# Moving the SBUF places of a split-precision decoder's matmul operands: weight high parts level with the streamed operand, low parts 64 bytes below it

## The chip, the cores and the metric

The kernel runs on one NeuronCore of a Trainium2 chip. The metric is the device time of one execution in microseconds (us). Before the change the median of three runs is 2209.86 us (2209.11 to 2210.26).

## What is computed

The reference is a small decoder trunk in float32: 256 positions, width 2048, two layers. Layer 0 mixes with sliding-window attention, layer 1 with a gated linear recurrence; each is followed by a gated feed-forward block of inner width 6144 with a three-tap causal convolution. Cut to the matrix products that matter here:

```python
def reference(x, ...):                       # x: (1, 256, 2048)
    for layer in range(2):
        h = rmsnorm(x, mix_norm[layer])
        if layer == 0:                       # qkv: 2048 -> 3072, w_o: 2048 -> 2048
            x = x + sliding_window_attention(h, w_qkv, q_gain, k_gain, sinks, w_o)
        else:                                # w_in: 2048 -> 4096, w_out: 2048 -> 2048
            x = x + rglru_block(h, w_in, conv_w, conv_b, w_a, b_a, w_i, b_i, lam, w_out)
        h = rmsnorm(x, ffn_norm[layer])      # w_up: 2048 -> 12288, w_down: 6144 -> 2048
        x = x + conv_ffn(h, w_up[layer], conv_w[layer], conv_b[layer], w_down[layer])
    return x
```

## The kernel before

**Split precision.** Every weight and every activation that TensorE multiplies is held as two parts: a high part (the value rounded to the matmul's input format, `F32R`) and a low part (the remainder). A product is the sum of high times high, high times activation-low and low times activation-high. The first two are one matmul: an activation row holds its high and its low part side by side (`h[P, KD, 2, T]`, 512 columns), so streaming the row through the high weights gives both sums in 512 PSUM columns. The third streams only the 256 high columns through the low weights.

**Chunks.** The weights are read in 372 chunks of 1 MB (128 partitions x 2048 numbers, 8192 bytes per partition) in one fixed order: `wk` 4, `wv` 4, `wq` 16, `wo` 16, then `wup` 96 and `wdn` 48 of layer 0, `win` 32, `wout` 16, and `wup` 96 and `wdn` 48 of layer 1. For each chunk SyncE's DMA queue loads `raw`; ScalarE copies it to `hi` (line 115); VectorE subtracts `hi` from `raw` and writes `lo` (line 123). There are three buffers each of `raw`, `hi` and `lo`. A call of `advance()` issues these three steps for the chunk that comes next. They sit between the groups of matmuls, so that each engine's program order interleaves them with the work on the results.

**Matmuls of a chunk.** A chunk holds 16 weight tiles of 128x128. TensorE loads a tile (a weight load) and streams the activation row past it (a matmul); while a matmul streams, the next tile is being loaded. `mm_hi` (line 189) streams 512 columns against `hi`, `mm_lo` (line 195) 256 columns against `lo`. In the stages `wup` (result `pu`), `win` (`px` and `py`), `wq` (`pq`), `wo` (`po`) and `wout` (`pr`) a chunk is a run of 16 matmuls of `mm_hi` and then a run of 16 of `mm_lo`; in `wq` the scores and transposes of the heads before stand inside the run of `mm_hi`. In `wdn` (`pd`) a chunk is 8 `mm_hi`, 8 `mm_lo`, 8 `mm_hi`, 8 `mm_lo`. The streamed operand is `h` for `wup`, `win` and `wq`, `g` (the gated inner values) for `wdn`, `z` (the gated recurrence) for `wout` and `ao` (the attention output) for `wo`.

**Where tiles lie.** Inside a partition the tiles lie one after another in the order in which the pools and tiles are declared, each start rounded up to 32 bytes. In what follows the place of a tile is its start byte modulo 256. A weight tile is 512 bytes, a row of a streamed operand 2048 bytes, a buffer 8192 bytes, so all tiles of a buffer, all three buffers and all rows of an operand have one place. Before the change `x` begins at byte 1152 and `h` at 17,536, which is place 128. The long-lived tiles of the pool `per` end with `sp`, `sp4` and `sp8` (64 bytes each, used for the recurrence's decay), and behind them come `raw`, `hi` and `lo`, and then everything that lives in one stage only, all from place 64 on:

| tile | start byte, before | place, before | place, after |
|---|---|---|---|
| `h` | 17,536 | 128 | 128 |
| `raw` (3) | 62,016 | 64 | 128 |
| `hi` (3) | 86,592 | 64 | 128 |
| `lo` (3) | 111,168 | 64 | 64 |
| `g`, `kz` (attention keys) | 135,744 | 64 | 128 |
| `vh` (attention values) | 152,128 | 64 | 128 |
| `ao` | 160,320 | 64 | 128 |
| `ghi`, `glo`, `xc` (gates) | 168,512, 172,608, 176,704 | 64 | 128 |
| `z` | 184,896 | 64 | 128 |
| `qh`, `pt` (attention, two each) | 218,624, 198,144 | 0 | 32 |

The lines that set this, and the two matmul helpers:

```python
per = ctx.enter_context(tc.tile_pool(name="per", bufs=1))
rawp = ctx.enter_context(tc.tile_pool(name="rawp", bufs=3))
hip = ctx.enter_context(tc.tile_pool(name="hip", bufs=3))
lop = ctx.enter_context(tc.tile_pool(name="lop", bufs=3))
...
pe.matmul(ps, lhsT=hi[:, off + k * n:off + k * n + P],
          rhs=rhs[:, xk].rearrange("p a t -> p (a t)"), ...)      # line 189
...
pe.matmul(ps[:, T:], lhsT=lo[:, off + k * n:off + k * n + P],
          rhs=rhs[:, xk, 0, :], ...)                              # line 195
```

Of the kernel before, what the change touches and what calls it, by code (L numbers as in the profile page):

```python
# [19 lines left out]
F32 = mybir.dt.float32  # L20
F32R = mybir.dt.float32r
AF = mybir.ActivationFunctionType
ALU = mybir.AluOpType
AX = mybir.AxisListType

P = 128
D = 2048
T = 256
KD = D // P
# [11 lines left out]
def trunk(ctx, tc, xT, wq, wk, wv, wo, win, wg, wout, wup, wdn, mixg, ffng, kqg, sinks,  # L41
# [3 lines left out]
    act, dve, pool, pe = nc.scalar, nc.vector, nc.gpsimd, nc.tensor  # L45

    def f(ap):
        return ap.bitcast(F32)

    per = ctx.enter_context(tc.tile_pool(name="per", bufs=1))  # L50
    rawp = ctx.enter_context(tc.tile_pool(name="rawp", bufs=3))
    hip = ctx.enter_context(tc.tile_pool(name="hip", bufs=3))
    lop = ctx.enter_context(tc.tile_pool(name="lop", bufs=3))
    ctx.enter_context(tc.manual_schedule())

    x = per.tile([P, KD, T], F32, name="x")
# [10 lines left out]
    fb = per.tile([P, 2, NT_UP], F32, name="fb")  # L67
    rw = per.tile([P, KD, 4], F32, name="rw")
    rbs = per.tile([P, 4, KD], F32, name="rbs")
    sp = per.tile([P, KD], F32, name="sp")  # L70
    sp4 = per.tile([P, KD], F32, name="sp4")
    sp8 = per.tile([P, KD], F32, name="sp8")


    order = []
# [91 lines left out]
    def rsqrt1(y, v):  # L167

        act.activation(out=y, in_=v, func=AF.Ln)
        act.activation(out=y, in_=y, func=AF.Exp, scale=-0.5)  # L170

    def rsqrt2(y, v, tmp):

        dve.tensor_tensor(out=tmp, in0=v, in1=y, op=ALU.mult)
        dve.scalar_tensor_tensor(out=tmp, in0=tmp, scalar=-0.5, in1=y, op0=ALU.mult, op1=ALU.mult)
        dve.scalar_tensor_tensor(out=y, in0=tmp, scalar=1.5, in1=y, op0=ALU.add, op1=ALU.mult)
# [102 lines left out]
    with ExitStack() as ph:  # L279
        ap_ = ph.enter_context(tc.tile_pool(name="attn", bufs=1, reuse_waits="tile"))  # L280
# [6 lines left out]
        kz = ap_.tile([P, 4, 2, 2, T], F32R, name="kz")  # L287
        vh = ap_.tile([P, 2, 2, 512], F32R, name="vh")
        ao = ap_.tile([P, KD, 2, T], F32R, name="ao")
        kq = ap_.tile([P, 1], F32, name="kq")  # L290
        kg = ap_.tile([P, 2], F32, name="kg")
        snk = ap_.tile([P, 32], F32, name="snk")
        nsnk = ap_.tile([P, 32], F32, name="nsnk")
        cb = ap_.tile([P, T], F32, name="cb")
# [72 lines left out]
        def k_fin(p):  # L367
            s, sq = ksq.pop(p)
            pk = psT.tile([P, 512], F32, tag="pT", name=f"pk{p}")
            pe.matmul(pk[:, 0:T], lhsT=bones, rhs=sq, start=True, stop=True)  # L370
            yield
            v = a2.tile([P, T], F32, tag="ka", name=f"kv{p}")
            r = a2.tile([P, T], F32, tag="kr", bufs=1, name=f"kr{p}")
            t = a2.tile([P, T], F32, tag="kt", bufs=1, name=f"kt{p}")
            dve.scalar_tensor_tensor(out=v, in0=pk[:, 0:T], scalar=1.0 / HD, in1=cb, op0=ALU.mult, op1=ALU.add)
            rsqrt1(r, v)
            yield
            rsqrt2(r, v, t)
            dve.scalar_tensor_tensor(out=s, in0=s, scalar=kq[:, 0:1], in1=r, op0=ALU.mult, op1=ALU.mult)
            for i in range(2):  # L380
                sl = slice(64 * i, 64 * i + 64)
                act.copy(out=kz[sl, p, 0, i, :], in_=s[sl])
                dve.tensor_tensor(out=kz[sl, p, 1, i, :], in0=s[sl], in1=f(kz[sl, p, 0, i, :]), op=ALU.subtract)
# [40 lines left out]
        for c in range(4):  # L424
            hi, lo = use()
            fin = k_fin(c)
            step(fin)
            for kk in range(4):
                k = 4 * c + kk
                for b in range(2):  # L430
                    tb = slice(b * P, b * P + P)
                    wsl = slice(kk * 512, kk * 512 + 512)
                    pe.matmul(pv[b], lhsT=h[:, k, 0, tb], rhs=hi[:, wsl], start=k == 0, stop=False)
                    pe.matmul(pv[b], lhsT=h[:, k, 1, tb], rhs=hi[:, wsl], start=False, stop=False)
                    pe.matmul(pv[b], lhsT=h[:, k, 0, tb], rhs=lo[:, wsl], start=False, stop=k == KD - 1)
            if c == 0:
                k_epi(3, psk[3])
            step(fin)
            dma_next()
            split_hi()  # L440
            if c:
                split_lo()
            finish(fin)
# [520 lines left out]
```

## Time and profile before

| | |
|---|---|
| median of three runs | 2209.86 us |
| the profiled execution | 2210.21 us |
| span of its instructions | 2208.4 us |
| TensorE busy with matmuls | 2184.8 us, 12,656 matmuls |
| VectorE, ScalarE, GpSimd busy | 1568.3, 1178.4, 153.3 us |
| granted TensorE clock over the span | 0.996 |
| read from HBM | 401.06 MB |

How to read it: busy times overlap, since the engines work side by side. Matmuls are pipelined, so the duration that the profile gives for one runs on into the next; the pace is the time from one start to the next, and the pace of a run of matmuls is the difference between the start of its first matmul and the start of the first one after it. The timeline of TensorE merges neighbouring matmuls of one kind: its first column is the start in us, the second the time until the last one of the group has ended, and x16 is their number.

### The profile page before, as it was taken

What the parts mean: (1) busy time and instruction counts of PE and PEld (TensorE: products, weight loads), DVE (VectorE), ACT (ScalarE), POOL (GpSimd) and SP (SyncE); (2) the same over time, 40 slices, a digit from 0 to 9 for tenths busy, and PEclk for the clock granted to TensorE, in tenths of its full rate; (3) what the DMA queues carried; (4) which work ended last, traced back from release to release, by engine and by line L of the source; (5) the groups of instructions that cost most, each with busy time, mean ns of one, the idle gap of its engine ahead of it and who ended that gap; (6) DMA issues with size and microseconds to landing.
All of it is one profiled execution on the core that took longest, in us unless ns stands there. A gap on an engine that the chain in (4) does not pass through costs nothing.

```text
span 2208.4 us, 30710 instructions
## 1 busy us (share of the span) xinstructions
PE 2184.8 (99%) x12656; PEld 1922.3 (87%) x12656; DVE 1568.3 (71%) x1877; ACT 1178.4 (53%) x1426; POOL 153.3 (7%) x140
## 2 busy tenths in 40 slices
PE   7999999999999999999999999999999999999999
PEld 6888888888888888888888888888888888888888
DVE  7877767777654777776678877777776457777644
ACT  4777445555433555553369874555554335555432
POOL 4122220000000000002200003100000000000000
PEclk9999999999999999999999999999999999999999
DMA  6333555555555555555445445455555555555543
GB/s 219 134 115 115 191 184 202 191 191 191 189 187 192 189 191 191 191 191 191 172 181 200 189 156 210 173 198 190 192 191 196 189 179 191 191 191 190 194 187 134
DMA packets 61051, 405.14 MB, mean 183 GB/s; under 512 B 7536, under 2 KB 9968, under 8 KB 13168
## 3 DMA queue, kind: packets, MB, share of 16 engines
q1 hardware_dynamic: 60912, 403.19, 51.1%
q8 instruction: 99, 1.62, 0.3%
q14 instruction: 40, 0.33, 0.0%
HBM read 401.06 MB, written 2.10 MB: 183 GB/s over the span
## 4 chain that ended last, share of the span: by engine, by line
PE 93%; DVE 3%; ACT 1%; DMA 1%; issue 1%; SPq 0%; DVEq 0%; ACTq 0%
PE pu L189 32%; PE pu L195 16%; PE pd L189 16%; PE pd L195 8%; PE pr L189 3%; PE po L189 3%; PE pq L189 2%; PE py L189 2%; PE px L189 1%; PE pr L195 1%; PE po L195 1%; PE pq L195 1%; PE py L195 1%; DMA raw<-in_win 1%; PE O L550 1%
## 5 line engine op out<-in xcount | busy, mean ns | idle before, releaser
L123 DVE TENSOR_TENSOR lo<-raw,hi 128x2048 fp32r<-128x2048 f32 (+1 forms) x390 | 857.2, 2198 | 220.5 <-ACT hi L115 212.6
L115 ACT CAST hi<-raw 128x2048 fp32r<-128x2048 f32 x373 | 712.7, 1911 | 394.9 <-PE pd L189 247.9
L189 PE MATMUL pu<-h,hi 128*128 128x512 f32 x3072 | 736.8, 392 | 0.0
L189 PEld LDWEIGHTS pu<-h,hi 128*128 128x128 f32 x3072 | 563.3, 188 | 110.9
L195 PEld LDWEIGHTS pu<-h,lo 128*128 128x128 f32 x3072 | 383.5, 188 | 16.4
L195 PE MATMUL pu<-h,lo 128*128 128x256 f32 x3072 | 387.1, 278 | 0.0
L189 PE MATMUL pd<-g,hi 128*128 128x512 f32 x1536 | 384.7, 392 | 0.0
L189 PEld LDWEIGHTS pd<-g,hi 128*128 128x128 f32 x1536 | 276.3, 189 | 49.2
L195 PEld LDWEIGHTS pd<-g,lo 128*128 128x128 f32 x1536 | 209.6, 191 | 15.0
L195 PE MATMUL pd<-g,lo 128*128 128x256 f32 x1536 | 214.3, 282 | 0.0
L672 ACT CAST g<-us 128x256 fp32r<-128x256 f32 x96 | 39.0, 407 | 280.7 <-DVE us L671 280.7
L665 DVE SCALAR_TENSOR_TENSOR uy<-us,fw,uy 128x255 f32<-128x255 f32 (+1 forms) x384 | 176.6, 481 | 6.8
L657 DVE TENSOR_TENSOR us<-pu,ua 128x512 f32<-128x512 f32 x96 | 66.4, 692 | 155.1 <-ACT ua L656 155.0
L656 ACT COPY ua<-pu 128x512 f32<-128x512 f32 x96 | 56.2, 586 | 144.0 <-PE pu L195 144.0
L662 ACT ACTIVATE uy<-us,fb,fw 128x256 f32<-128x256 f32 x192 | 105.2, 599 | 2.7 <-DVE us L658 2.7
L203 DVE TENSOR_TENSOR xt<-pd,x 128x512 f32<-128x512 f32 (+1 forms) x40 | 23.3, 583 | 82.2 <-PE pd L195 82.2
L160 POOL TENSOR_TENSOR sqt<-x 128x512 f32<-128x512 f32 x28 | 64.5, 2304 | 179.7 <-DVE x L204 176.6
L673 DVE TENSOR_TENSOR g<-us,g 128x256 fp32r<-128x256 f32 x96 | 40.9, 426 | 45.3 <-ACT g L672 45.3
L158 POOL TENSOR_TENSOR sqa<-x 128x512 f32<-128x512 f32 x4 | 8.3, 2070 | 916.2 <-DVE x L204 915.6
L189 PE MATMUL pq<-h,hi 128*128 128x512 f32 x256 | 71.3, 403 | 0.2 <-DVE vh L448 0.2
L658 DVE TENSOR_TENSOR us<-us,rb 128x512 f32<-128x512 f32 x96 | 66.5, 692 | 3.3
L189 PE MATMUL po<-ao,hi 128*128 128x512 f32 x256 | 62.3, 392 | 1.1 <-DVE ao L560 1.1
(195 smaller groups left out, 1908.7 us busy)
## 6 DMA issues: line engine op xcount, KB each, us to landing
raw<-in_wup SPq DMA_DIRECT2D x192, 1024.0 KB, 4.8
raw<-in_wdn SPq DMA_DIRECT2D x96, 1024.0 KB, 4.8
raw<-in_win SPq DMA_DIRECT2D x32, 1024.0 KB, 5.6
raw<-in_wq SPq DMA_DIRECT2D x16, 1024.0 KB, 4.8
raw<-in_wo SPq DMA_DIRECT2D x16, 1024.0 KB, 4.8
raw<-in_wout SPq DMA_DIRECT2D x16, 1024.0 KB, 4.8
raw<-in_wv SPq DMA_DIRECT2D x4, 1024.0 KB, 5.3
graw<-in_wg SPq DMA_DIRECT2D x8, 512.0 KB, 3.3
```

The source lines that it names most:

```text
L115: act.copy(out=his[c], in_=raws[c])
L123: dve.tensor_tensor(out=los[c][:, part], in0=raws[c][:, part], in1=f(his[c][:, part]), op=ALU.subtract)
L160: pool.tensor_tensor(out=sqt, in0=src, in1=src, op=ALU.mult)
L189: pe.matmul(ps, lhsT=hi[:, off + k * n:off + k * n + P], rhs=rhs[:, xk].rearrange("p a t -> p (a t)"), start=start and k == ks[0][0], stop ...
L195: pe.matmul(ps[:, T:], lhsT=lo[:, off + k * n:off + k * n + P], rhs=rhs[:, xk, 0, :], start=False, stop=stop and k == ks[-1][0])
L656: act.copy(out=a, in_=ps[:, :, 0:T])
L657: dve.tensor_tensor(out=s, in0=ps[:, :, T:], in1=a, op=ALU.add)
L658: dve.tensor_tensor(out=s, in0=s, in1=rbb, op=ALU.mult)
L662: act.activation(out=y[:, i, :], in_=s[:, i, :], func=AF.Identity, scale=fw[:, layer, n, 2:3], bias=fb[:, layer, n:n + 1])
L665: dve.scalar_tensor_tensor(out=y[:, i, tap:], in0=s[:, i, 0:T - tap], scalar=fw[:, layer, n, 2 - tap:3 - tap], in1=y[:, i, tap:], op0=ALU. ...
L672: act.copy(out=g[:, m, 0, :], in_=s[:, 0, :])
L673: dve.tensor_tensor(out=g[:, m, 1, :], in0=s[:, 0, :], in1=f(g[:, m, 0, :]), op=ALU.subtract)
```

## The change

Two small pools are put between the weight pools. `sp`, `sp4` and `sp8` (192 bytes) move out of `per` into `gap0`, which lies between `hi` and `lo`, and an unused tile of 64 bytes in `gap1` lies behind `lo`. With that `raw` and `hi` begin 192 bytes lower (place 128), `lo` stays where it was (place 64), and all stage tiles begin 64 bytes higher (place 128). To make room for it at the top end of the partition, the one-number tile `kq` is dropped; its value (the product of the two gains) is written over the first column of `kg`, which is not read afterwards. No instruction is added, removed or moved on any engine's queue; of the names in them only `kq` becomes `kg`.

```diff
     hip = ctx.enter_context(tc.tile_pool(name="hip", bufs=3))
+    gap0 = ctx.enter_context(tc.tile_pool(name="gap0", bufs=1))
     lop = ctx.enter_context(tc.tile_pool(name="lop", bufs=3))
+    gap1 = ctx.enter_context(tc.tile_pool(name="gap1", bufs=1))
 ...
-    sp = per.tile([P, KD], F32, name="sp")
-    sp4 = per.tile([P, KD], F32, name="sp4")
-    sp8 = per.tile([P, KD], F32, name="sp8")
+    sp = gap0.tile([P, KD], F32, name="sp")
+    sp4 = gap0.tile([P, KD], F32, name="sp4")
+    sp8 = gap0.tile([P, KD], F32, name="sp8")
+    gap1.tile([P, 16], F32, name="pad")
 ...
-        kq = ap_.tile([P, 1], F32, name="kq")
         kg = ap_.tile([P, 2], F32, name="kg")
+        kq = kg[:, 0:1]
 ...
-            dve.scalar_tensor_tensor(out=s, in0=s, scalar=kq[:, 0:1], in1=r, op0=ALU.mult, op1=ALU.mult)
+            dve.scalar_tensor_tensor(out=s, in0=s, scalar=kq, in1=r, op0=ALU.mult, op1=ALU.mult)
```

In terms of the distance from the streamed operand's place to the weights' place:

| stage | streamed | `hi`, before | `lo`, before | `hi`, after | `lo`, after |
|---|---|---|---|---|---|
| `wup`, `win`, `wq` (240 chunks) | `h` | -64 | -64 | 0 | -64 |
| `wdn`, `wout`, `wo` (128 chunks) | `g`, `z`, `ao` | 0 | 0 | 0 | -64 |

## The prediction

> **What bounds the kernel now.** I read the page's first parts, then the chain that ended last, then TensorE's timeline stage by stage.
>
> ```profile
> span 2208.4 us, 30710 instructions
> PE 2184.8 (99%) x12656; PEld 1922.3 (87%) x12656; DVE 1568.3 (71%) x1877; ACT 1178.4 (53%) x1426; POOL 153.3 (7%) x140
> ...
> PEclk9999999999999999999999999999999999999999
> ...
> PE 93%; DVE 3%; ACT 1%; DMA 1%; issue 1%; SPq 0%; DVEq 0%; ACTq 0%
> PE pu L189 32%; PE pu L195 16%; PE pd L189 16%; PE pd L195 8%; PE pr L189 3%; PE po L189 3%; PE pq L189 2%; PE py L189 2%; PE px L189 1%; PE pr L195 1%; PE po L195 1%; PE pq L195 1%; PE py L195 1%; DMA raw<-in_win 1%; PE O L550 1%
> ```
>
> TensorE is busy for 99% of the span at an almost full granted clock, and 93% of the chain is its matmuls, lines 189 and 195 above all. It does not wait for data; the pace at which matmuls follow one another is the time. A change of addresses can act only through that pace, or by making another engine so slow that TensorE waits. So the question is whether the pace depends on where the weights lie against the streamed operand. The kernel before holds two such distances, so its own timeline can be asked. First `wup`, where `hi` and `lo` lie 64 bytes below `h`:
>
> ```profile
> 331.15 3.13 PE L189 MATMUL pu<-h,hi 128*128 128x512 f32 x13
> ...
> 386.31 3.82 PE L189 MATMUL pu<-h,hi 128*128 128x512 f32 x16
> 389.97 2.05 PE L195 MATMUL pu<-h,lo 128*128 128x256 f32 x16
> 391.86 3.84 PE L189 MATMUL pu<-h,hi 128*128 128x512 f32 x16
> 395.53 1.98 PE L195 MATMUL pu<-h,lo 128*128 128x256 f32 x16
> 397.35 3.82 PE L189 MATMUL pu<-h,hi 128*128 128x512 f32 x16
> ...
> 562.85 3.82 PE L189 MATMUL pu<-h,hi 128*128 128x512 f32 x16
> ```
>
> Start to start, the runs of `hi` take 3.66 and 3.67 us, those of `lo` 1.89 and then 1.82: two paces that take turns. From 331.15 to 562.85 there are 42 chunks, so one takes 5.517 us. Next `wdn`, whose distance is 0 for both parts:
>
> ```profile
> 572.06 1.98 PE L195 MATMUL pu<-h,lo 128*128 128x256 f32 x16
> 573.88 2.00 PE L189 MATMUL pd<-g,hi 128*128 128x512 f32 x8
> 575.72 1.12 PE L195 MATMUL pd<-g,lo 128*128 128x256 f32 x8
> ...
> 587.84 2.00 PE L189 MATMUL pd<-g,hi 128*128 128x512 f32 x8
> 589.68 1.12 PE L195 MATMUL pd<-g,lo 128*128 128x256 f32 x8
> 590.63 2.00 PE L189 MATMUL pd<-g,hi 128*128 128x512 f32 x8
> ...
> 596.22 2.00 PE L189 MATMUL pd<-g,hi 128*128 128x512 f32 x8
> ```
>
> Eight `hi` take 1.84 us and eight `lo` 0.95; three such halves from 587.84 to 596.22 give 2.793 each. Per matmul `lo` costs 119 ns here, against 118 and 113 in `wup`. And `wout`, distance 0, in the same runs of 16 as `wup`:
>
> ```profile
> 1326.72 3.82 PE L189 MATMUL pr<-z,hi 128*128 128x512 f32 x16
> 1330.38 2.08 PE L195 MATMUL pr<-z,lo 128*128 128x256 f32 x16
> 1332.29 3.82 PE L189 MATMUL pr<-z,hi 128*128 128x512 f32 x16
> ...
> 1399.09 3.14 PE L189 MATMUL pr<-z,hi 128*128 128x512 f32 x13
> ```
>
> From 1326.72 to 1399.09 there are 13 chunks of 5.567 us, 3.655 for `hi` and 1.912 for `lo`. So of two runs that are alike but for the distance, `hi` is a little quicker at 0 (3.655 against 3.665), and `lo` clearly quicker at -64 (1.82 to 1.89 against 1.91). The change gives every stage the 0 for `hi` and the -64 for `lo`.
>
> **The change part by part.** The sum is made against the profiled execution's 2210.21 us (span 2208.4 and 1.8 around it), which is 0.35 above the median of the runs.
>
> What is unknown is one number: how long a run of 16 `lo` at -64 takes when the run of `hi` before it had distance 0. No row shows that order. It is bounded by the two paces of `wup`, 1.815 and 1.885; I take their mean, 1.85, since in the nearest rows each follows a run of `hi` equally often, and keep both for the range. With 3.655 for `hi` a chunk takes 5.505 us (5.47 to 5.54). That `hi` at 0 keeps its pace behind a run of `lo` at -64 is shown: the first half-chunk of `wdn`, behind the `lo` of `wup`, takes 573.88 to 575.72, the same 1.84 as later ones.
>
> - `wup`, 192 chunks: 5.517 to 5.505 is -0.012 each, -2.3 us (ends: -9.0 and +4.4).
> - `wdn`, 192 half-chunks: only `lo` changes, from 0.952 (2.793 less 1.841) to half of 1.85, -0.027 each, -5.2 us (-8.6, -1.9).
> - `wo` and `wout`, 32 chunks: 5.567 to 5.505, -2.0 us (-3.1, -0.9).
> - `win`, 32 chunks, where a third pace of `hi` shows:
>
> ```profile
> 1140.59 3.90 PE L189 MATMUL px<-h,hi 128*128 128x512 f32 x16
> 1144.32 2.05 PE L195 MATMUL px<-h,lo 128*128 128x256 f32 x16
> 1146.21 3.83 PE L189 MATMUL py<-h,hi 128*128 128x512 f32 x16
> ...
> 1204.17 3.84 PE L189 MATMUL py<-h,hi 128*128 128x512 f32 x16
> ...
> 1209.66 3.82 PE L189 MATMUL py<-h,hi 128*128 128x512 f32 x16
> ...
> 1215.21 3.84 PE L189 MATMUL px<-h,hi 128*128 128x512 f32 x16
> ```
>
> Chunks of 5.62, 5.49 and 5.55 us, 5.55 on the mean, become 5.505: -1.4 us (-2.6, -0.3).
> - `wq`, 16 chunks, whose run of `hi` is cut up by the scores:
>
> ```profile
> 203.27 2.02 PE L189 MATMUL pq<-h,hi 128*128 128x512 f32 x8
> 205.13 0.50 PE L472 MATMUL S<-bones,qsq 128*128 128x2 f32 x4
> ...
> 209.48 2.05 PE L195 MATMUL pq<-h,lo 128*128 128x256 f32 x16
> 211.37 1.22 PE L550 MATMUL O<-pt,vh 128*128 128x256 f32 x9
> ```
>
> `lo` goes from 1.89 to 1.85 and the first eight `hi` from 1.86 to 1.84, -0.06 a chunk, -1.0 us (-1.5, -0.3).
>
> The sum is -11.9 us (-24.8 to +1.0).
>
> Taken at nothing: the matmuls of scores and values, 17 for each of 16 steps, whose `pt` and `qh` go from place 0 to 32. If each went from the quickest pace of 256 columns seen (113 ns) to the slowest (119) or back, that is 272 times 6 ns, +-1.6 us; there is no reason for a sign. `wk` and `wv` are 8 chunks in a stretch that starts with the first loads; +-0.5 by the same paces. Writing the gain over `kg` costs nothing: the same three kinds of VectorE instruction stand in the same order. The splits, whose operands now lie at 128 and 64 rather than all at 64:
>
> ```profile
> L123 DVE TENSOR_TENSOR lo<-raw,hi 128x2048 fp32r<-128x2048 f32 (+1 forms) x390 | 857.2, 2198 | 220.5 <-ACT hi L115 212.6
> L115 ACT CAST hi<-raw 128x2048 fp32r<-128x2048 f32 x373 | 712.7, 1911 | 394.9 <-PE pd L189 247.9
> ...
> raw<-in_wup SPq DMA_DIRECT2D x192, 1024.0 KB, 4.8
> ```
>
> They are covered: VectorE needs 2.2 us for its split in a chunk of 5.5 and is 71% busy in all, and ScalarE waits most of its idle time for a matmul to release `hi`. If a split took 10% longer it would still lie beside the matmuls. A load takes 4.8 us and three buffers are in flight, so a chunk that is 0.05 shorter finds its data.
>
> So 2210.2 - 11.9 = 2198.3, and against the median 2198.0 us, 0.5% faster.
>
> **The rivals.**
>
> *The `lo` all keep the pace of 1.89.* Whether a run of `lo` takes 1.82 or 1.89 is settled by what the run of `hi` before left behind: in the rows of `wup` 1.89 follows the `hi` run of 3.66, and 1.82 the one of 3.67. The runs of `hi` at 0 are all alike (3.655), so they may give every run of `lo` one and the same pace. If it is 1.885, the sum is its upper end, +1.0: 2210.9, no change. If it is 1.815, it is the lower end, 2185.1. For the slow one speaks that the quicker run of `hi` is the one followed by it, and 3.655 is nearest to that; against it, that the two paces are equally frequent.
>
> *The place is not the cause.* `wdn`, `wo` and `wout` differ from `wup` in the streamed operand too, and `wdn` in its runs of 8. Then only noise is left: 2209.9. Against it: `wo` and `wout` share all with `wup` but the place, other engines' traffic differs between the stages and the runs repeat to 0.01 us all the same. The Trainium skill has this rule, in TensorE: Matmul & The Clock Gate, section Part 2: What happens when you issue a matmul: the streamed operand and the weight load have read ports of their own, and loading the next weights takes no read bandwidth from the running matmul. By that rule the distance would be free and the time 2209.9; the trace of before does not bear it out, 119 ns against 113 for the same 256 columns.
>
> *Slower: `hi` at its new places takes its longest pace.* In the first row of `win` a run of `hi` takes 3.73 us. The 3.655 was seen with `hi` an even number of 256-byte steps away from `g`, `ao` and `z` (192, 288, 384); now it is an odd number from every operand (193, 289, 385, and 269 from `h`). If what counts repeats every 512 bytes and not every 256, the new distance has never been seen. Priced with that pace: a chunk of 5.62 us (the row pair 1140.59 to 1146.21) instead of 5.517 in `wup`, +0.103 x 192 = +19.8; +0.014 for each half-chunk of `wdn`, +2.7; +0.053 and +0.07 for the 32 chunks each of `wo`/`wout` and `win`, +3.9; `wq` +0.5. In sum +26.9, 2236.8. It decides from 3.69 us a run on, where 372 runs eat up the 11.9 us.
>
> **How the numbers follow.** A run within 0.2% (4.4 us) counts as no change. The forecast, with its `lo` anywhere from 1.815 to just above the mean, 0.46; all `lo` at 1.885, 0.29; the place is not the cause, 0.09; `hi` at 3.73, 0.16. So faster 0.46, same 0.38, slower 0.16. The forecast's own range is 2184 to 2204; the two cases without a change end at 2211, and with +-2 us for attention and the first chunks the range is 2182 to 2215. The `hi` at 3.73 is left out.
>
> **What would show it.** In the timeline after the change: runs of 16 `hi` at 3.65 to 3.66 in every stage, `win` included, with no 3.73; runs of `lo` at 1.82 to 1.89, and eight of `wdn` at 0.91 to 0.94 and no longer 0.95; TensorE still at 99%, weight splits at 2198 and 1911 ns. All runs of `lo` at 1.89 would be the first rival; `lo` at 1.91 in `wout` the second; `hi` above 3.69 the third. If the splits grew and TensorE showed idle time before line 195, the reasoning on the cover would be wrong.

## The result, and the profile after

The median of four runs is 2224.34 us (2223.8 to 2224.78) against 2209.49 us of the kernel before beside them: a ratio of 1.0070 (95% interval 1.0056 to 1.0084). The change makes the kernel 0.7% slower; the forecast was 0.5% faster, and its range ended 9 us below the result. The profiled execution took 2224.45 us. In its page the lines of code have numbers that are five higher than before (the matmuls of `mm_hi` are line 194, those of `mm_lo` line 200). First the span, TensorE's busy time, the chain that ended last, and the two groups of the weight splits:

```profile
span 2222.6 us, 30710 instructions
PE 2199.0 (99%) x12656; PEld 1925.2 (87%) x12656; DVE 1568.0 (71%) x1877; ACT 1177.4 (53%) x1426; POOL 153.5 (7%) x140
...
PE 94%; DVE 2%; ACT 2%; DMA 1%; issue 1%; SPq 0%; ACTq 0%; DVEq 0%
...
L128 DVE TENSOR_TENSOR lo<-raw,hi 128x2048 fp32r<-128x2048 f32 (+1 forms) x390 | 857.0, 2198 | 221.4 <-ACT hi L120 220.4
L120 ACT CAST hi<-raw 128x2048 fp32r<-128x2048 f32 x373 | 712.1, 1910 | 401.2 <-PE pd L194 252.8
```

The span grew by 14.2 us (2208.4 to 2222.6) and TensorE's busy time by the same 14.2 (2184.8 to 2199.0); its idle time is 23.6 us in both. The splits cost what they cost before (2198 and 1910 ns), so the cover held and no new wait appeared: the matmuls themselves follow one another more slowly. Where, TensorE's timeline tells (start, time until the last of the group has ended), `wup` first and then `wdn`:

```profile
320.38 3.80 PE L194 MATMUL pu<-h,hi 128*128 128x512 f32 x16
324.01 2.05 PE L200 MATMUL pu<-h,lo 128*128 128x256 f32 x16
325.89 3.85 PE L194 MATMUL pu<-h,hi 128*128 128x512 f32 x16
329.58 2.05 PE L200 MATMUL pu<-h,lo 128*128 128x256 f32 x16
...
571.12 3.85 PE L194 MATMUL pu<-h,hi 128*128 128x512 f32 x16
...
576.69 2.04 PE L194 MATMUL pd<-g,hi 128*128 128x512 f32 x8
578.56 1.11 PE L200 MATMUL pd<-g,lo 128*128 128x256 f32 x8
...
596.39 2.03 PE L194 MATMUL pd<-g,hi 128*128 128x512 f32 x8
```

From 325.89 to 571.12 there are 44 chunks of 5.573 us, where there were 5.517. The two paces that took turns are gone: all 188 runs of 16 `lo` in `wup` take 1.88 or 1.89, the slower of the two, and 186 of the 188 runs of `hi` 3.69, longer than either pace of before (3.66 and 3.67) and longer than at distance 0 in the old `wout` (3.655). In `wdn` eight `hi` take 1.87 and a half-chunk 2.814 ((596.39 - 576.69) / 7), where it took 2.793. `wout`, whose `hi` stayed at distance 0 and where the distance of `lo` alone changed:

```profile
1339.42 3.85 PE L194 MATMUL pr<-z,hi 128*128 128x512 f32 x16
1343.11 2.05 PE L200 MATMUL pr<-z,lo 128*128 128x256 f32 x16
1344.99 0.40 PE L194 MATMUL pr<-z,hi 128*128 128x512 f32 x1
```

The `lo` got quicker, as forecast (1.88 for 1.91), and the `hi`, whose distance is the same, slower (3.69 for 3.655): 5.57 as before. So per chunk `wup` gives 192 x 0.056 = 10.8 us, `wdn` 192 halves x 0.021 = 4.0, `wo` and `wout` 0.2: 15.0 us by these rows, where 14.2 were measured. That it is the two feed-forward blocks, half each, the starts of the first and of the stage behind it show (of before, then of after):

```profile
308.08 0.63 PE L189 MATMUL pu<-h,hi 128*128 128x512 f32 x2
...
1106.98 0.87 PE L189 MATMUL px<-h,hi 128*128 128x512 f32 x3
```
```profile
308.38 0.87 PE L194 MATMUL pu<-h,hi 128*128 128x512 f32 x3
...
1114.29 0.88 PE L194 MATMUL px<-h,hi 128*128 128x512 f32 x3
```

The block of layer 0 takes 805.91 us for 798.90, 7.0 more, and nearly nothing is lost before it (0.3). The recurrence between the blocks takes 297.58 us for 297.67, and the block of layer 1 with the end 810.7 for 803.7, again 7.0 more.

### The profile page after: what moved, and what is told of

Its sections match the earlier page's. It is cut to its first block, busy times and chain, and to the rows that moved or that the text cites. A ratio compares the mean times of both kernels' runs of the same rounds, so it can differ in the third digit from the quotient of the medians.

```text
span 2222.6 us, 30710 instructions
## 1 busy us (share of the span) xinstructions
PE 2199.0 (99%) x12656; PEld 1925.2 (87%) x12656; DVE 1568.0 (71%) x1877; ACT 1177.4 (53%) x1426; POOL 153.5 (7%) x140
## 4 chain that ended last, share of the span: by engine, by line
PE 94%; DVE 2%; ACT 2%; DMA 1%; issue 1%; SPq 0%; ACTq 0%; DVEq 0%
PE pu L194 32%; PE pu L200 16%; PE pd L194 16%; PE pd L200 8%; PE pr L194 3%; PE po L194 3%; PE pq L194 2%; PE py L194 2%; PE px L194 1%; PE pr L200 1%; PE po L200 1%; PE pq L200 1%; PE py L200 1%; DMA raw<-in_win 1%; PE O L555 1%
## 5 line engine op out<-in xcount | busy, mean ns | idle before, releaser
L128 DVE TENSOR_TENSOR lo<-raw,hi 128x2048 fp32r<-128x2048 f32 (+1 forms) x390 | 857.0, 2198 | 221.4 <-ACT hi L120 220.4
L120 ACT CAST hi<-raw 128x2048 fp32r<-128x2048 f32 x373 | 712.1, 1910 | 401.2 <-PE pd L194 252.8
L200 PEld LDWEIGHTS pu<-h,lo 128*128 128x128 f32 x3072 | 389.2, 188 | 15.0
L200 PE MATMUL pu<-h,lo 128*128 128x256 f32 x3072 | 393.8, 279 | 0.0
L194 PE MATMUL pd<-g,hi 128*128 128x512 f32 x1536 | 390.6, 396 | 0.0
```

What stands on the lines that cost most here:

```text
L120: act.copy(out=his[c], in_=raws[c])
L128: dve.tensor_tensor(out=los[c][:, part], in0=raws[c][:, part], in1=f(his[c][:, part]), op=ALU.subtract)
L194: pe.matmul(ps, lhsT=hi[:, off + k * n:off + k * n + P], rhs=rhs[:, xk].rearrange("p a t -> p (a t)"), start=start and k == ks[0][0], stop ...
```

## Experiments

The theories at the start: **P**, the time is set by TensorE's pace, and that by the distance of `hi` and of `lo` (place of the weights less place of the streamed operand, modulo 256) and by the run that went before; against it **D**, what counts repeats every 512 bytes, or `hi` is slow at its new places for another reason.

**Undo one half: all at distance 0.** `hi` and the streamed operands stay where the change put them, `lo` follows to place 128.

```diff
     hip = ctx.enter_context(tc.tile_pool(name="hip", bufs=3))
-    gap0 = ctx.enter_context(tc.tile_pool(name="gap0", bufs=1))
     lop = ctx.enter_context(tc.tile_pool(name="lop", bufs=3))
+    gap0 = ctx.enter_context(tc.tile_pool(name="gap0", bufs=1))
```

> hi and lo both at distance 0 from every streamed operand (hi an odd number of 256-byte steps away, as after the change). Theory P (the pace of a run follows from its distance modulo 256 and from how the run before it ended): the up stage takes the pace that wout had before, 3.655 + 1.912 = 5.567 us a chunk, wdn 2.793 a half-chunk as before; against before +0.050 x 192 = +9.6 us, about 2219 to 2220. Theory D (the change was slower because hi now lies an odd number of 256-byte steps away): hi keeps the 3.689 of after, 5.60 us a chunk, 1.870 + 0.952 in wdn, about 2234.

2219.8 us, ratio to before 1.0042 (1.0028 to 1.0057). TensorE's timeline in `wup`, with a last row from a window that starts inside a run, so that its last eight matmuls stand alone:

```profile
442.90 3.82 PE L194 MATMUL pu<-h,hi 128*128 128x512 f32 x16
446.56 2.08 PE L200 MATMUL pu<-h,lo 128*128 128x256 f32 x16
448.47 3.82 PE L194 MATMUL pu<-h,hi 128*128 128x512 f32 x16
...
444.75 1.98 PE L194 MATMUL pu<-h,hi 128*128 128x512 f32 x8
```

Here `hi` and all streamed operands stand at the very addresses of the changed kernel, and the run of `hi` is back at 3.66. So the 3.69 does not come from the place of `hi` alone; it comes with the place of the `lo` that goes before. The same cut through a run of the changed kernel, and through its first full run, which follows only two `lo`:

```profile
327.76 1.99 PE L194 MATMUL pu<-h,hi 128*128 128x512 f32 x8
...
322.43 1.75 PE L194 MATMUL pu<-h,hi 128*128 128x512 f32 x7
```

From 325.89 to 327.76 the first eight take 1.87 us, the last eight (to 329.58) 1.82; with `lo` at distance 0 it is 1.85 and 1.81. The settled pace is the same, 226 to 227 ns a matmul (seven in 1.58 from 322.43 to 324.01), and what differs is an entry of some ten matmuls at the start of each run. The differences between single starts, in ns and with their sum at the end, show it:

```
changed kernel, 325.89   241 236 234 236 224 231 236 228 233 231 226 227 227 226 227 226   3689
changed kernel, 320.38   232 230 228 226 227 227 226 227 227 226 227 227 226 226 228 226   3636
all at 0, 442.90         234 235 229 232 231 226 227 227 227 226 227 227 226 226 228 226   3654
before, wdn, 573.88      231 236 229 232 231 227 226 226                                   1838
before, wout, 1315.58    231 231 235 228 233 231 227 226 227 227 226 226 228 226           3202
changed, wout, 1322.76   241 237 234 235 225 230 236 229 232 231 227 226 227 226           3236
```

The last two rows show that the distances and the slow pace of the `lo` in front do not settle the entry. They are the first runs of `wout`, behind the last `lo` of `win` (of before, then of after):

```profile
1313.70 2.05 PE L195 MATMUL py<-h,lo 128*128 128x256 f32 x16
1315.58 3.37 PE L189 MATMUL pr<-z,hi 128*128 128x512 f32 x14
...
1320.88 2.05 PE L200 MATMUL py<-h,lo 128*128 128x256 f32 x16
1322.76 3.40 PE L194 MATMUL pr<-z,hi 128*128 128x512 f32 x14
```

In both kernels `hi` at distance 0 stands here behind 16 slow `lo` (1.88) at -64, and yet the 14 matmuls take 3.20 us before and 3.24 after. Two things differ. Before, the weights of both runs lie at place 64 and the streamed operand goes from 128 (`h`) to 64 (`z`); after, the operand stays at 128 and the weights go from 64 to 128. And the run of `hi` in front of that `lo` had distance -64 before and 0 after. No run here separates the two. So theory P, the distances and the run before, is not the whole of it.

**Undo the other half: all at distance -64.** `sp`, `sp4` and `sp8` go back into `per`, so `hi` returns to place 64; the pad of 64 bytes behind `lo` stays, and so the streamed operands of all stages lie at 128.

```diff
-    sp = gap0.tile([P, KD], F32, name="sp")
-    sp4 = gap0.tile([P, KD], F32, name="sp4")
-    sp8 = gap0.tile([P, KD], F32, name="sp8")
+    sp = per.tile([P, KD], F32, name="sp")
+    sp4 = per.tile([P, KD], F32, name="sp4")
+    sp8 = per.tile([P, KD], F32, name="sp8")
```

> hi and lo both 64 bytes below every streamed operand. P: chunks of 5.517 us as in the up stage before, in wo and wout too (from 5.567, -0.050 x 32 = -1.6 us); wdn's half-chunk unknown between 2.73 (1.83 + 0.90) and 2.81 (1.87 + 0.94); 2196 to 2212, 2207 if wdn stays as it was. D says nothing against before's up stage: 2209 as well.

2200.25 us, ratio 0.9957 (0.9942 to 0.9972): better than both kernels. `wup` is as before the change, and `wdn` has its two paces now too (the page, then the timeline):

```profile
span 2198.2 us, 30710 instructions
PE 2174.2 (99%) x12656; PEld 1912.0 (87%) x12656; DVE 1567.9 (71%) x1877; ACT 1178.6 (54%) x1426; POOL 153.6 (7%) x140
...
440.01 3.82 PE L193 MATMUL pu<-h,hi 128*128 128x512 f32 x16
443.67 2.04 PE L199 MATMUL pu<-h,lo 128*128 128x256 f32 x16
445.55 3.84 PE L193 MATMUL pu<-h,hi 128*128 128x512 f32 x16
449.23 1.98 PE L199 MATMUL pu<-h,lo 128*128 128x256 f32 x16
451.04 3.82 PE L193 MATMUL pu<-h,hi 128*128 128x512 f32 x16
...
574.24 1.11 PE L199 MATMUL pd<-g,lo 128*128 128x256 f32 x8
575.18 2.00 PE L193 MATMUL pd<-g,hi 128*128 128x512 f32 x8
577.01 1.07 PE L199 MATMUL pd<-g,lo 128*128 128x256 f32 x8
577.92 1.99 PE L193 MATMUL pd<-g,hi 128*128 128x512 f32 x8
```

Eight `lo` take 0.94 and 0.91 in turn, and a half-chunk 2.757 on the mean: 0.036 less than before, 192 times, is 6.9 us. So the loss comes with the move of `hi` (and `raw` with it): with `lo` and the operands where the change has them and `hi` back at -64, the kernel is 24 us quicker.

**The fourth corner: `hi` at -64, `lo` at 0.**

```diff
-    gap1 = ctx.enter_context(tc.tile_pool(name="gap1", bufs=1))
 ...                                    # sp, sp4, sp8 back into per
+    gap0.tile([P, 16], F32, name="pad")
```

> The reverse of the change: hi 64 bytes below, lo at the operand's place. P: lo at 1.912 in every stage; hi somewhere between the three paces of -64 seen before (3.66, 3.68, 3.735), so 5.57 to 5.65 us a chunk, 2220 to 2236. If the paces were sums of independent prices of the two distances (theory S), hi 3.667 + lo 1.912 = 5.58, about 2221.

2221.32 us, ratio 1.0052 (1.0037 to 1.0067).

```profile
442.65 3.84 PE L193 MATMUL pu<-h,hi 128*128 128x512 f32 x16
446.32 2.08 PE L199 MATMUL pu<-h,lo 128*128 128x256 f32 x16
448.24 3.84 PE L193 MATMUL pu<-h,hi 128*128 128x512 f32 x16
```

`lo` takes 1.92 here and the chunk 5.59. In the other half of `wup` (from 716 us, and again from 1819) the runs hold to another order, 3.660 and 1.913, so that a chunk takes 5.583 on the mean. That is the sum which theory S expected (5.58 us, 2221): this kernel alone speaks for independent prices. The four corners, for a chunk of `wup` and a half-chunk of `wdn`:

| `hi` | `lo` | `hi` + `lo` of a chunk, us | half-chunk, us | kernel, us |
|---|---|---|---|---|
| 0 | 0 | 3.655 + 1.912 | 2.793 | 2219.8 |
| 0 | -64 (the change) | 3.689 + 1.884 | 2.814 | 2224.3 |
| -64 | -64 | 3.668 + 1.849 | 2.757 | 2200.25 |
| -64 | 0 | 3.668 + 1.915 | 2.786 | 2221.3 |

All four together speak against it. If the prices of `hi` and `lo` simply added up, the two corners with equal distances would have the same sum as the two mixed ones; they have 11.084 us and 11.156, so the two interact.

**An even number of 256-byte steps.** The third rival of the prediction blamed the odd number of 256-byte steps between `hi` and the operands. Here 256 bytes more lie behind `hi` instead of in front of it, so that `hi` is an even number of steps away from `g`, `z` and `ao`, with all places modulo 256 as in the changed kernel.

```diff
-    gm = per.tile([P, 2, KD], F32, name="gm")
-    gf = per.tile([P, 2, KD], F32, name="gf")
+    gm = gap0.tile([P, 2, KD], F32, name="gm")
+    gf = gap0.tile([P, 2, KD], F32, name="gf")
```

> The change, with hi and raw 256 bytes lower: the places modulo 256 are those of after, but hi lies an even number of 256-byte steps from h, g, ao and z, as from g, ao and z before. P: nothing changes, 3.689 + 1.884 a chunk, 2224. D: hi goes back to 3.655 and 1.841, 2209.

2224.5 us, ratio 1.0063 (1.0048 to 1.0078), with the changed kernel's runs of 3.69 and 1.88. For `hi`, the odd or even number of steps makes no difference; with the run at distance 0 above, both halves of D fall.

**Fewer entries.** If the loss is an entry per run of `hi`, `wdn` must win by having half as many. In the changed kernel its two groups of 8 `hi` are put together, then its two groups of 8 `lo`:

```diff
                         for i in range(2):
                             mm_hi(ps[:, i], hi, g, ks, off=i * P, n=2 * P, start=c == 0)
+                        for i in range(2):
                             mm_lo(ps[:, i], lo, g, ks, off=i * P, n=2 * P, stop=c == 2)
```

> The changed kernel, with the two eights of hi in a wdn chunk put behind one another, and then the two eights of lo: runs of 16. P (a run of hi at distance 0 pays a fixed entry behind lo at -64, some ten matmuls long, and then keeps 226.6 ns): hi 3.689 a chunk for 2 x 1.870, lo 1.884 for 2 x 0.943, -0.053 x 96 = -5 us, 2219. If the cost were per matmul (233.8 ns, theory M): no change, 2224.

2219.7 us, ratio to before 1.0045 (1.0028 to 1.0062), 4.6 us less than the changed kernel: 96 entries of 0.05 us.

```profile
592.31 3.85 PE L194 MATMUL pd<-g,hi 128*128 128x512 f32 x16
596.00 2.05 PE L200 MATMUL pd<-g,lo 128*128 128x256 f32 x16
```

**Another distance: all weights 128 away.** Of the three tiles `sp8` alone moves, and it lies behind `lo` with the pad.

```diff
-    sp8 = gap0.tile([P, KD], F32, name="sp8")
+    sp8 = gap1.tile([P, KD], F32, name="sp8")
 ...                                    # sp and sp4 back into per
```

> hi and lo both 128 bytes away from every streamed operand, runs of 16 and 8 as before. P says only that the pace depends on the distance and that both parts lie in the span seen: hi 226 to 235 ns, lo 113 to 120 ns, 2180 to 2240 us. If only 64 bytes below were special (theory 64), it runs as distance 0, 2220.

2237.05 us in a single run, so without an interval: the longest of all, where 2220 was expected if only 64 bytes below were special.

```profile
440.17 3.88 PE L193 MATMUL pu<-h,hi 128*128 128x512 f32 x16
443.88 2.06 PE L199 MATMUL pu<-h,lo 128*128 128x256 f32 x16
445.78 3.90 PE L193 MATMUL pu<-h,hi 128*128 128x512 f32 x16
```

Runs of `hi` take 3.71 to 3.73 us, those of `lo` 1.90, and a chunk 5.62 on the mean. Runs of `hi` as long as the one of 3.73 that the prediction saw in `win` exist steadily, but at a distance that the change doesn't make.

**What decides between 1.88 and 1.81 at distance -64.** Single starts of the kernel with all at -64 (ns):

```
hi, 440.01   226 229 232 226 229 232 226 229 231 226 229 232 226 229 232 226   then lo 117 118 118 ... 1884
hi, 445.55   233 235 230 232 226 229 231 226 229 232 226 229 232 226 229 231   then lo 114 113 113 ... 1814
```

`hi` goes through a cycle of three paces, 226, 229, 232; a run of `lo` is quick when the run of `hi` before it ended on the third. Sixteen is not a multiple of three, so a run that begins the cycle ends one step too far, and the next, with its irregular entry, ends right. Two kernels tried to end every run on the third step by cutting `wup` and `wdn` across chunks, into runs of 15, 18, 15 and of 17, 17, 14; for this a weight chunk is prepared one step earlier.

```diff
-            mm_hi(ps[:, i], hi, h, rng(0, KD))
-            mm_lo(ps[:, i], lo, h, rng(0, KD))
+            # the second kernel: n matmuls of hi, then the same n of lo
+            n = min((17, 17, 14)[r % 3], len(items) - p)
```

> e2's places (hi and lo 64 bytes below every streamed operand), but in the feed-forward blocks the runs are cut at 15, 18 and 15 matmuls over three chunks, no longer at 16 (and 8), and one more chunk is split ahead. Theory P (what decides between 1.81 and 1.885 us for sixteen lo is where in a cycle of three paces, 225, 230 and 232 ns, the run of hi ends): behind quick lo a run of hi starts with 226 and a length that 3 divides ends behind 232, so every lo run is quick: 113.3 ns a matmul, hi 229, 5.48 us for a chunk's worth, up stages -0.04 x 192 = -7.5 and down stages -0.036 x 96 = -3.5 us against e2: about 2189. Rival R (the alternation follows the buffers or the chunks' parity): lo goes on alternating, 2200 as e2 or a little more.

> As e5, but the runs are 17, 17 and 14 matmuls long, none of which 3 divides. P: no run of hi started behind quick lo ends at the right place of the cycle, so most or all lo run at 117.8 ns: 5.55 us a chunk's worth, against e2's 5.517 and 5.513 some +0.035 x 288 = +10 us: 2205 to 2212. R, or a gain from the extra chunk of lead or from fewer, longer runs: as e5.

Both were slower than the uncut kernel: 2227.63 us (1.0073, 1.0053 to 1.0092) and 2225.35 us (1.0071, 1.0056 to 1.0086). The page and the timeline of the first:

```profile
span 2227.4 us, 30713 instructions
PE 2184.8 (98%) x12656; PEld 1919.3 (86%) x12656; DVE 1555.4 (70%) x1877; ACT 1162.7 (52%) x1426; POOL 127.6 (6%) x140
...
447.02 3.60 PE L193 MATMUL pu<-h,hi 128*128 128x512 f32 x15
450.45 1.93 PE L199 MATMUL pu<-h,lo 128*128 128x256 f32 x15
452.22 3.60 PE L193 MATMUL pu<-h,hi 128*128 128x512 f32 x15
```

Against the uncut kernel the span grew by 29.2 us (2198.2 to 2227.4). The starts of the stages show where: `win`, whose runs were not cut, takes 229.1 us for 207.9, and `wout`, not cut either, 93.9 for 88.3. TensorE's waits for `xc` before the gates' matmuls sum up to 19.4 us for 4.6, and before `wout` there is one of 3.6 for `z`. The second kernel loses the same there (227.3 and 93.7). So the cover failed behind the feed-forward block of layer 0; which part of the new order VectorE and ScalarE owe this to was not taken apart.

The feed-forward blocks show the paces. In layer 0 the block takes 4.7 us more than uncut: 15 `lo` take 1.77, the slow pace, since behind a slow `lo` these runs begin at the cycle's second step, 229, and 15 of them end on 226. In layer 1, and already from 990 us on, the runs begin with 226, 15 `lo` take 1.70 as expected, and the block takes 3.0 us less than uncut. The cuts of 17, 17, 14 got quick and slow runs in turn and cost nothing in the blocks, where 10 us more were expected.

So the cuts were next put inside a chunk, where nothing else moves: 16 orders in one kernel, in blocks of 12 chunks.

```diff
-                            mm_hi(ps[:, i], hi, h, rng(0, KD))
-                            mm_lo(ps[:, i], lo, h, rng(0, KD))
+                            for a, b in zip(cuts, cuts[1:]):
+                                mm_hi(ps[:, i], hi, h, rng(a, b), start=a == 0)
+                                mm_lo(ps[:, i], lo, h, rng(a, b), stop=b == KD)
```

> All weights 64 bytes below the streamed operands, as in the kernel that ran at 2200.25 us, and in wup the run of a chunk is cut in two (for instance 15 hi, 15 lo, 1 hi, 1 lo) at another point in each of 16 blocks of 12 chunks, so that one trace shows 16 orders. Nothing is left out. Theory P (a run of lo is quick, 113 ns, when the run of hi before it ended on the third pace of the cycle 226, 229, 232; each run of hi starts with 226 behind a quick lo and with 229 behind a slow one): cuts at 14 in every chunk give 14 quick lo and two slow ones, 3.66 + 1.82 = 5.48 us a chunk; cuts at 15 in every second chunk give a little under 5.50; cuts at 13 and 11 give 5.52 and more. In sum 2195 to 2205 us, since most blocks don't have the best cut. Rival R (each change from hi to lo and back costs a fixed 0.05 us, whatever the phase): every cut chunk is 0.05 us longer, 5.57, about 130 cut chunks, 2207 us, and no block is under 5.51.

2202.6 us in one run. The expectation for cuts at 14 was wrong (5.540 us a chunk: the run of 14 begins with 226 and ends on 229, so that its 14 `lo` are slow, and only the two `lo` behind the run of 2 are quick), and so was that for cuts at 11 (5.500 us, where 5.52 and more was expected). The same cut gives different paces by the run that it follows: 15 and 1 in every second chunk, entered behind slow `lo`, took 5.570 and 5.557, and entered behind quick ones 5.477 and 5.490. Both orders keep themselves up over a whole block; where two cut chunks follow each other, at 375.81 us, the slow one turns into the quick one. A fixed price for each change from `hi` to `lo` (rival R) is out, since the cut chunk of the quick order is the quickest of all.

**The best order everywhere.** All at -64, with every second chunk cut into 15 and 1 from a point at which a run begins with 226, in `wup`, `wdn`, `wout` and most of `wo`:

```diff
+    def cut_chunk(cut, hi_part, lo_part):
+        for a, b in (((0, 15), (15, 16)) if cut else ((0, 16),)):
+            hi_part(a, b)
+            lo_part(a, b)
```

> All weights 64 bytes below the streamed operands; in wup, wdn, wout and from the sixth chunk of wo on, every second chunk runs 15 hi, 15 lo, 1 hi, 1 lo and the other one 16 hi, 16 lo (wdn with the matmuls of both column blocks in one run). Nothing is left out. The block of the kernel with 16 orders that ran so took 5.477 and 5.490 us a chunk in turn. Theory P (the paces of the runs carry over from stage to stage, and only the point at which a run of hi ends counts): 5.4835 us a chunk in all of them, so against the uncut kernel's 2200.25 us 188 x 0.0335 = 6.3 in wup, 96 x 0.030 = 2.9 in wdn, 0.9 in wo and wout: 2190 us, 2188 to 2193. Rival R (the good order needs the start that it had there and falls into the slow lock, 5.570 and 5.557, at a stage's beginning): 0.047 us a chunk more than uncut in the stages that miss it; with wdn or one half of wup missing, 2196 to 2205, with all missing 2214.

2191.16 us, ratio to before 0.9924 (0.9911 to 0.9938): the quickest of the study, 33 us below the changed kernel.

```profile
450.85 3.60 PE L193 MATMUL pu<-h,hi 128*128 128x512 f32 x15
454.29 1.86 PE L199 MATMUL pu<-h,lo 128*128 128x256 f32 x15
455.99 0.39 PE L193 MATMUL pu<-h,hi 128*128 128x512 f32 x1
...
456.33 3.84 PE L193 MATMUL pu<-h,hi 128*128 128x512 f32 x16
460.01 1.98 PE L199 MATMUL pu<-h,lo 128*128 128x256 f32 x16
461.82 3.36 PE L193 MATMUL pu<-h,hi 128*128 128x512 f32 x14
```

But for one pair at the start of layer 1, all runs of 15 and 16 `lo` in `wup` are quick (1.70 and 1.81), and two chunks take 10.97 us (450.85 to 461.82), 5.485 each. The sum of the expectation, 2190, is 1 us off.

## Why the prediction was wrong

- *What bounds the kernel*: right. The time is TensorE's pace, and all of the difference lies in lines 194 and 200.
- *The place counts* (second rival: it doesn't): right. Five pairs of distances give chunks of `wup` from 5.517 to 5.62 us, and `wdn` takes 2.793 a half-chunk at distance 0 whether both places are 64 (before) or 128. The Trainium skill, in TensorE: Matmul & The Clock Gate, section Part 2: What happens when you issue a matmul, says that the weight load and the streamed operand have independent read ports and that the load steals nothing from a running matmul; these traces do not agree, 3.654 to 3.73 us for the same 16 matmuls of 512 columns. Whether the read ports are the reason, no run shows.
- *`hi` at 0 keeps its pace behind `lo` at -64, and that is shown*: **this is the step that failed.** The row it rested on (573.88 to 575.72, 1.84 us) stands where `wup` passes to `wdn`: there the streamed operand changes and the weights stay at place 64. The change brings another order, in which the operand stays and the weights go from place 64 (`lo`) to 128 (`hi`) in every chunk, and of that order no row existed. In it `hi` pays the longer entry, 3.689 for 3.655 and 1.87 for 1.84. The `lo` in front of 573.88 had moreover the quick pace, and the changed kernel has the slow one throughout; but the row of 1315.58, behind a slow `lo`, has the short entry too, so the slow pace alone is not the reason. By the sum's terms that is 0.034 x 256 + 0.029 x 192 = 14.3 us of the miss of 26.1 (-11.9 forecast, +14.2 measured), a little too much, since a third of the runs in `win` keep 3.65.
- *`lo` takes the mean, 1.85*: wrong in size. It takes the slower bound, 1.884, throughout: 0.034 x 256 + 0.018 x 192 = 12.2 us. The first rival had this and its reason, that like runs of `hi` leave one and the same pace behind; by its price alone the time would have been 2210.9.
- *The third rival*, `hi` above 3.69 at its new places: right in direction, half of its price (+14.2 for +26.9), wrong in cause. Its premise, an odd number of 256-byte steps, made no difference when it was undone (2224.5 us), and with `hi` at the very same places and `lo` at 0 the run is back at 3.66.
- *The bounds*: "5.47 to 5.54" for a chunk took the best and worst `lo` but one value of `hi`. With `hi` as unknown as `lo`, up to the 3.73 that a row showed, the range would have held the time.
- *Covered work* (splits at other places, the gain written over `kg`): right, 2198 and 1910 ns and no new wait. Attention and the first chunks, given +-2 us, moved 0.3 us by 308.38.

What stays open is the mechanism inside: why a run of `lo` at -64 leaves a longer entry for `hi` at 0 than `lo` at 0 does, why it did not at 1315.58, and why the last step of the cycle sets the pace of the next run. The runs show what happens at these distances and shapes, not its cause. Other distances (64 above, or `hi` and `lo` at different ones of them) were not tried.

## What to carry to other kernels

When a change brings two parts into a new order, a pace read from a row holds only for the neighbour that it had there, and a row at the border of two stages, where the operand changes too, does not stand for the same order inside a stage: before calling it shown, look at what ran ahead of it, and give each part that has a new neighbour its own bounds. Where TensorE is busy for 99% of the span, compare runs of the same matmul start to start over the stages; differences of 1 to 2% can come from the places of weights and streamed operand modulo 256, and one unused tile of 64 bytes is a cheap thing to try (0.4% here, 0.8% with the order fitted to it). Measure all corners of such a layout, since the best value for each part taken alone was the worst corner of the four here.

## What the runs showed of the hardware

- In this kernel the distance between the starts of weights and streamed operand modulo 256 goes with the pace of the matmuls: for 512 columns 226.7 ns settled at 0, and 229 on the mean of a cycle of three at -64; for 256 columns 119.5 ns with both parts at 0, and 113.3 or 117.8 with both at -64.
- The pace has a memory. A run's first ten matmuls, and at -64 the pace of the whole next run, depend on the runs before; two self-sustaining orders of the same cuts, 15 and 1 in every second chunk, differed by 0.08 us a chunk (5.4835 against 5.5635).
- In steady stretches these sequences repeat to 1 or 2 ns from chunk to chunk, and they carry over from stage to stage: with all at -64 and the cuts, the quick order goes on from `wup` into `wdn`.
